# Memory layer: the sample rows of both feature blocks stacked and turned by one transpose

## The chip, the cores and the metric

The kernel runs on one NeuronCore of a Trainium2 chip. The metric is the device time of one execution in microseconds (us), the median of several runs. All inputs, outputs and arithmetic are fp32; matrix products are made from split operands (below).

## The reference, cut to what matters

One inference step of a two-layer decoder runs over 320 tokens: a prompt of 256 tokens and a sample group of 8 sequences with 8 new tokens each (64 tokens). Layer 0 is a gated MLP over chunks, layer 1 is an mLSTM (a matrix memory with 8 heads, key width 128, value width 256), and each layer is followed by a convolutional feed-forward block. The change touches the end of each head of the mLSTM, where its output is normalised over the 256 value features, gated and handed to the output projection:

```
num = w_inter * (q @ C) + sc @ v
den = w_inter * (q @ n) + sum(sc)
h   = num / max(|den|, exp(-m_t))
hn  = (h - mean(h)) * rsqrt(var(h) + EPS) * gn_g      # over the 256 features of a head
y   = (sigmoid(o_pre) * hn) @ w_out
```

## The kernel before, in words

**Layout.** The residual stream lies with features on the 128 partitions and the 320 tokens along the free axis: columns 0 to 255 are the prompt, columns 256 to 319 the sample (`TP` = 256, `T` = 320). Every projection is made of blocks of 128 output features: `block` (L185) multiplies eight 128x128 weight tiles with the 320 token columns. Weights and activations are split in a high part (`wh`, `xh`, `yhb`) and a low part (`wl`, `xl`, `ylb`), and a product is three matmuls: high-high, high-low, low-high. In the memory layer `chunk` (L173) first makes the 16 matmuls with `wh`, then the 8 with `wl`.

**The weight stream.** A list `wq` (L65 to L114) names the weights in the order of their use. `take` (L165) hands out the next one and calls `prefetch` (L120): the raw weight four places ahead is loaded by a DMA of SyncE (SP) into one of four `raw` buffers, and the next one is split in one of three pairs of buffers: ScalarE (ACT) makes `wh` (L154), VectorE (DVE) makes `wl` = `raw` - `wh` (L155).

**The heads.** The loop over 8 heads `h` (L1025) is software-pipelined: in iteration `h`, the projections of head `h` alternate on TensorE (PE) with the remaining steps of head `h`-1. In the order of PE: q block, `inter` (products with the state C), k block, `numer` (the numerators: two PSUM tiles for the prompt rows, one for the sample), first v block, `state_prompt`, `state_sample` 0, second v block, `state_sample` 1, `scores` of head `h`, first o block, **`finish` of head `h`-1**, `state_sample` 2, second o block, `state_sample` 3, `k_nat`, `v_nat` (transposes of k and v), `inter(h, 0)`. In the heads below, "finish(h)" is the step for head `h`; finish(0) to finish(6) stand in iterations 1 to 7, finish(7) after the loop. Beside these stand blocks of the output projection (`early`), wherever their operands are ready.

**The last head.** The output projection's inputs from heads 4 to 7 come late, so three of its blocks are begun in pieces by `begin` (L1016). Weight pieces of 4, 4, 2 and 2 tiles (L101 to L103) are taken in iteration 7 and just behind the loop, and the order of PE there is:

```
h = NH - 1
begin(0)        # 2 tiles
begin(1)        # 2 tiles
inter(h, 1)
for i in (2, 3):
    inter(h, i)
numer(h)
ps = blk()
```

**The step that is changed.** `stats` (L898) has token rows on the partitions. For the two prompt tiles (128 rows each) the numerators stay in PSUM; for the sample, ACT and DVE sum two halves into `ns` (64 rows x 258, SBUF). It computes mean and variance (DVE), a power -1/2 (POOL, L919), a scale `sl` and a bias `nb` (DVE, L922, L926), and then ACT writes the normalised rows to `hn` (128 x 3 x 256): one instruction for each of three token tiles, the third with 64 rows (L929). Rows 64 to 127 of the third tile are zeros, written once (L998). `finish` (L968) turns `hn` back: for each of the two feature blocks `e`, three 128x128 transposes on PE (`tr`, L975) into one PSUM tile `phn`, of which columns 0 to 319 are used; DVE multiplies them with the gate (L977, `y_b`), ACT makes `yhb` (L979), DVE `ylb` (L980).

**What sets the order.** Every matmul and transpose is pinned: PE works in the order of the program. On the other engines and on the DMA queue of SP a list scheduler of the framework decides, when the kernel is built, in which order the instructions are issued; each engine then works through its list strictly in that order, and waits where an operand is not ready. Only a few instructions beside PE's are pinned or told what to follow (`behind_split`, L160; `between`, L1092). PSUM tiles come from two rings: `psm` with three tiles for blocks, `psa` with five for everything else (`phn` among them); a tile of a ring is given out again after its last reader.

Of the kernel before, what the change touches and what calls it, by code (L numbers as in the profile page):

```python
# [10 lines left out]
F32 = mybir.dt.float32  # L11
F32R = mybir.dt.float32r
AF = mybir.ActivationFunctionType
ALU = mybir.AluOpType
MULT, ADD, SUB, MAX = ALU.mult, ALU.add, ALU.subtract, ALU.max

P = 128
EPS = 1e-6
TP = 256
NB, NS = 8, 8  # L20
T = TP + NB * NS
# [6 lines left out]
DV = 256  # L28
# [9 lines left out]
class Net:  # L38
# [576 lines left out]
    def layer_b(self):  # L615
        nc, tc, I, O = self.nc, self.tc, self.I, self.O
# [4 lines left out]
        with ExitStack() as ctx:  # L621
# [276 lines left out]
            def stats(h, between=None):  # L898
                s = S[h]
                num, mv, dn = s.pop("num"), mvs[h % 2], dns[h % 2]  # L900
                ns = hp.tile([64, CW], F32, tag="ns", name="ns", bufs=1)
                nc.scalar.copy(ns, num[2][64:, :CW])
                nc.vector.tensor_tensor(ns, num[2][:64, :CW], ns, op=ADD)
                src = [num[0], num[1], ns]
                bst = hp.tile([P, 3, 6], F32, tag="bstat", name="bstat", bufs=1)
                for t in range(3):
                    n = P if t < 2 else 64
                    nc.vector.bn_stats(bst[:n, t, :], src[t][:n, :DV])
                    nc.vector.bn_aggr(mv[:n, t, :], bst[:n, t:t + 1, :])
                    nc.scalar.activation(dn[:n, t:t + 1], src[t][:n, DV:DV + 1], AF.Abs)  # L910
                rd = hp.tile([P, 3], F32, tag="rd", name="rd", bufs=1)
                nc.vector.tensor_tensor(rd, dn, colsT[:, :, 64 + h], op=MAX)
                nc.vector.reciprocal(rd, rd)
                t1 = hp.tile([P, 3], F32, tag="t1", name="t1", bufs=1)
                nc.vector.tensor_tensor(t1, mv[:, :, 1], rd, op=MULT)
                nc.vector.tensor_tensor(t1, t1, rd, op=MULT)
                nc.vector.tensor_scalar(t1, t1, EPS, None, op0=ADD)
                sl = hp.tile([P, 3], F32, tag="sl", name="sl", bufs=1)
                made = nc.gpsimd.tensor_tensor(sl, t1, self.mhalf.to_broadcast([P, 3]), op=ALU.pow)  # L919
                if between:  # L920
                    between(made)
                mul = nc.vector.tensor_tensor(sl, sl, rd, op=MULT)  # L922
                if between:
                    self.pin(mul)
                nb = hp.tile([P, 3], F32, tag="nb", name="nb", bufs=1)
                nc.vector.scalar_tensor_tensor(nb, mv[:, :, 0], -1.0, sl, op0=MULT, op1=MULT)  # L926
                for t in range(3):
                    n = P if t < 2 else 64
                    nc.scalar.activation(hn[:n, t, :], src[t][:n, :DV], AF.Identity, scale=sl[:n, t:t + 1], bias=nb[:n, t:t + 1])  # L929

            def state_prompt(h):
                s = S[h]
# [35 lines left out]
            def finish(h):  # L968
                s = S[h]
                yh = hp.tile([P, 2, T], F32R, tag="yhb", name="yhb", bufs=6)  # L970
                yl = hp.tile([P, 2, T], F32R, tag="ylb", name="ylb", bufs=6)
                for e in range(2):
                    pt = self.psa.tile([P, 512], F32, tag="pa", name="phn")
                    for t in range(3):
                        self.tr(pt[:, t * P:(t + 1) * P], hn[:, t, e * P:(e + 1) * P], self.ident)  # L975
                    y = self.tp.tile([P, T], F32, tag="yf", name="y_b", bufs=2)
                    nc.vector.scalar_tensor_tensor(y, s["o"][e], 1.0, pt[:, :T], op0=ADD, op1=MULT)  # L977
                    g = gnh[:, 2 * h + e:2 * h + e + 1]
                    nc.scalar.activation(yh[:, e, :], y, AF.Copy, scale=g)  # L979
                    nc.vector.scalar_tensor_tensor(yl[:, e, :], y, g, yh[:, e, :].bitcast(F32), op0=MULT, op1=SUB)  # L980
                    Y[2 * h + e] = (yh[:, e, :], yl[:, e, :])
# [8 lines left out]
            hp = ctx.enter_context(tc.tile_pool(name="hb", bufs=1))  # L990
# [2 lines left out]
            Qz = hp.tile([P, 8 * 136], F32R, name="Qz")  # L993

            Ps = hp.tile([P, P], F32R, name="Ps")
            hn = hp.tile([P, 3, DV], F32, name="hn")
            nc.gpsimd.memset(Ps.bitcast(F32), 0.0)
            nc.gpsimd.memset(hn[64:, 2, :], 0.0)  # L998
            nc.gpsimd.memset(vh[:, :, DV:DV + 1].bitcast(F32), 1.0)
            nc.gpsimd.memset(vh[:, :, DV + 1:].bitcast(F32), 0.0)  # L1000
            nc.gpsimd.memset(vl[:, :, DV:].bitcast(F32), 0.0)
# [23 lines left out]
            for h in range(NH):  # L1025
                if h:
                    qk_epi(h, 0, blk())
                    early(h, 0)
                    if h == 1:
                        inter(0, 0)  # L1030
                        state_split(0, 3)
                    inter(h - 1, 1)
                    qk_epi(h, 1, blk())
                    for i in (2, 3):
                        inter(h - 1, i)
                    numer(h - 1)
                    early(h, 1)
                    ps = blk()
                    with self.behind_split():
                        stats(h - 1)  # L1040
                    v_epi(h, 0, ps)
                    state_prompt(h - 1)
                    state_sample(h - 1, 0)
                    early(h, 2)
                    v_epi(h, 1, blk())
# [7 lines left out]
                if h:  # L1053
                    finish(h - 1)
# [37 lines left out]
            def between(made):  # L1092
                with tc.issue_after(made.ins):
                    k_mask(h)
                o_epi(h, 0, ps)

            stats(h, between)
            state_prompt(h)
            o_epi(h, 1, blk())
            finish(h)  # L1100
            for i in range(4):
                state_sample(h, i)
# [159 lines left out]
```

## Time and profile before

| | before |
|---|---|
| median of 3 runs | 965.59 us (965.24 to 965.87) |
| profiled execution, its own time | 965.17 us |
| its span, first to last instruction | 963.4 us |
| mean granted TensorE clock | 0.997 of full speed |
| transposes into `phn` | 48, six for each head |
| normalised sample rows `hn<-ns` (L929) | 8 of 64x256, 595 ns each |
| gate product `y_b` (L977) | 16 of 128x320, 475 ns each |
| memory layer's heads on PE | about 450 us to 704 us of the span |

A row of a timeline or of the chain reads: start in us from the span's start, duration in us, engine, line, operation, out<-in. Durations of neighbours on an engine overlap, since instructions are pipelined: what one costs its queue is the distance from its start to the next start, here called its pitch. PE is TensorE's matmul and transpose, PEld its weight load, which runs ahead of the matmul that uses it. SPq is the DMA queue of SyncE.

### The profile page before, as it was taken

What the parts mean: (1) busy time and instruction counts of PE and PEld (TensorE: products, weight loads), DVE (VectorE), ACT (ScalarE), POOL (GpSimd) and SP (SyncE); (2) the same over time, 40 slices, a digit from 0 to 9 for tenths busy, and PEclk for the clock granted to TensorE, in tenths of its full rate; (3) what the DMA queues carried; (4) which work ended last, traced back from release to release, by engine and by line L of the source; (5) the groups of instructions that cost most, each with busy time, mean ns of one, the idle gap of its engine ahead of it and who ended that gap; (6) DMA issues with size and microseconds to landing.
All of it is one profiled execution on the core that took longest, in us unless ns stands there. A gap on an engine that the chain in (4) does not pass through costs nothing.

```text
span 963.4 us, 17284 instructions
## 1 busy us (share of the span) xinstructions
PE 954.8 (99%) x6495; PEld 942.1 (98%) x6495; DVE 700.8 (73%) x1364; ACT 518.0 (54%) x946; POOL 114.0 (12%) x288
## 2 busy tenths in 40 slices
PE   9999999999999999999999999999999999999997
PEld 8889999999999999999999999999999999999997
DVE  6766976587777755469999988787887777775443
ACT  7557444455555443358676756565665455444341
POOL 2200000010000000024322212102101000000000
PEclk9999999999999999999999999999999999999998
DMA  8643356544444455564465654554474444445441
GB/s 274 208 145 132 130 153 192 166 135 151 153 154 147 143 166 149 152 225 144 150 200 183 188 189 162 186 171 125 131 239 137 153 154 153 153 138 160 141 139 55
DMA packets 58505, 154.83 MB, mean 161 GB/s; under 512 B 7782, under 2 KB 20326, under 8 KB 58422
## 3 DMA queue, kind: packets, MB, share of 16 engines
q1 hardware_dynamic: 58422, 153.74, 50.3%
q8 instruction: 51, 0.84, 0.4%
q14 instruction: 32, 0.26, 0.1%
HBM read 141.78 MB, written 11.94 MB: 160 GB/s over the span
## 4 chain that ended last, share of the span: by engine, by line
PE 97%; DVE 2%; ACT 1%; issue 0%; DVEq 0%; POOL 0%; ACTq 0%
PE pm L54 81%; PE pv_a L54 6%; PE num L54 3%; PE pcs L54 2%; PE pmix L54 1%; PE psc L54 1%; PE pCp L54 1%; PE pv L57 1%; PE phn L57 1%; DVE wl L155 0%; PE pw L54 0%; PE pc L54 0%; PE pk L57 0%; DVE yo L610 0%; ACT wh L154 0%
## 5 line engine op out<-in xcount | busy, mean ns | idle before, releaser
L154 ACT CAST wh<-raw 128x1024 fp32r<-128x1024 f32 (+3 forms) x256 | 256.9, 1004 | 299.6 <-PE pm L54 150.0
L155 DVE TENSOR_TENSOR wl<-raw,wh 128x1024 fp32r<-128x1024 f32 (+3 forms) x256 | 298.9, 1168 | 116.2 <-ACT wh L154 112.1
L54 PE MATMUL pm<-xh,wh 128*128 128x320 f32 x1216 | 372.3, 311 | 0.0
L54 PE MATMUL pm<-xl,wh 128*128 128x320 f32 x1216 | 370.3, 309 | 0.0
L54 PE MATMUL pm<-xh,wl 128*128 128x320 f32 x1216 | 321.1, 309 | 0.0
L54 PEld LDWEIGHTS pm<-xl,wh 128*128 128x128 f32 x1216 | 228.3, 188 | 0.2
L54 PEld LDWEIGHTS pm<-xh,wh 128*128 128x128 f32 x1216 | 228.3, 188 | 0.2
L54 PEld LDWEIGHTS pm<-xh,wl 128*128 128x128 f32 x1216 | 214.5, 188 | 0.0
L54 PE MATMUL pm<-yh_f,wh 128*128 128x320 f32 x352 | 108.8, 309 | 0.0
L54 PE MATMUL pm<-yl_f,wh 128*128 128x320 f32 x352 | 108.8, 309 | 0.0
L54 PE MATMUL pm<-yh_f,wl 128*128 128x320 f32 x352 | 108.8, 309 | 0.0
L54 PEld LDWEIGHTS pm<-yh_f,wh 128*128 128x128 f32 x352 | 66.1, 188 | 0.0
L54 PEld LDWEIGHTS pm<-yl_f,wh 128*128 128x128 f32 x352 | 66.1, 188 | 0.0
L54 PEld LDWEIGHTS pm<-yh_f,wl 128*128 128x128 f32 x352 | 66.1, 188 | 0.0
L531 DVE SCALAR_TENSOR_TENSOR fcv<-fpad,vecs,fcv 128x336 f32<-128x336 f32 x88 | 49.6, 565 | 2.1 <-ACT fcv L529 0.6
L303 DVE TENSOR_TENSOR xT<-pm,xT 128x320 f32<-128x320 f32 x39 | 19.1, 490 | 33.5 <-PE pm L54 33.1
L54 PE MATMUL pm<-yh_a,wh 128*128 128x320 f32 x128 | 39.6, 310 | 0.0
L54 PE MATMUL pm<-yh_a,wl 128*128 128x320 f32 x128 | 39.5, 309 | 0.0
L54 PE MATMUL pm<-yl_a,wh 128*128 128x320 f32 x128 | 39.5, 309 | 0.0
L533 ACT ACTIVATE fgl<-fcv 128x256 f32<-128x256 f32 x44 | 18.2, 415 | 37.8 <-DVE fcv L531 37.8
L54 PE MATMUL pm<-yhb,wh 128*128 128x320 f32 x128 | 38.1, 311 | 0.0
L54 PE MATMUL pm<-ylb,wh 128*128 128x320 f32 x128 | 37.9, 309 | 0.0
(290 smaller groups left out, 1399.0 us busy)
## 6 DMA issues: line engine op xcount, KB each, us to landing
raw<-in_f_up SPq DMA_DIRECT2D x88, 512.0 KB, 3.3
raw<-in_b_win SPq DMA_DIRECT2D x48, 512.0 KB, 3.6
raw<-in_f_dn SPq DMA_DIRECT2D x32, 448.0 KB, 3.3
C<-in_C SPq DMA_DIRECT2D x32, 258.0 KB, 3.6
raw<-in_a_win SPq DMA_DIRECT2D x16, 512.0 KB, 3.3
raw<-in_a_wo SPq DMA_DIRECT2D x16, 512.0 KB, 3.9
raw<-in_f_dn SPq DMA_DIRECT2D x16, 512.0 KB, 3.5
out_Cs<-C SPq DMA_DIRECT2D x32, 256.0 KB, 2.8
```

Source lines behind the costliest of these rows:

```text
L54: self.pin(self.nc.tensor.matmul(out, lhsT, rhs, start=start, stop=stop, skip_group_check=skip))
L57: self.pin(self.nc.tensor.transpose(out, in_, ident))
L154: self.last_split = self.hold(nc.scalar.copy(wh[:, :kn, :], raw[:, :kn, :]))
L155: self.last_low = nc.vector.tensor_tensor(wl[:, :kn, :], raw[:, :kn, :], wh[:, :kn, :].bitcast(F32), op=SUB)
L303: self.nc.vector.tensor_tensor(x, ps[:, :T], x, op=ADD)
L531: nc.vector.scalar_tensor_tensor(cv, pd[:, i:i + NC], self.vec(w + i * KF), cv, op0=MULT, op1=ADD)
L533: nc.scalar.activation(gl[:, :TP], cv[:, :TP], AF.Gelu_apprx_tanh)
```

## The change

The sample rows of a head are 64 tokens x 256 features. Before, they are one 64x256 tile, padded with zero rows to 128, and cost one transpose in each feature block. After, ACT writes them in two halves into a tile `hs` of 128x128: features 0 to 127 on partitions 0 to 63, features 128 to 255 on partitions 64 to 127. One transpose of `hs` gives both blocks side by side in columns 256 to 383 of the first `phn` tile (`p0`). The second block's gate product is made in two: its 64 sample columns from `p0`, its 256 prompt columns from its own tile. The zero fill is gone.

```diff
@@ stats
-                for t in range(3):
-                    n = P if t < 2 else 64
-                    nc.scalar.activation(hn[:n, t, :], src[t][:n, :DV], AF.Identity, scale=sl[:n, t:t + 1], bias=nb[:n, t:t + 1])
+                for t in range(2):
+                    nc.scalar.activation(hn[:, t, :], src[t][:, :DV], AF.Identity, scale=sl[:, t:t + 1], bias=nb[:, t:t + 1])
+
+                for e in range(2):
+                    nc.scalar.activation(hs[64 * e:64 * e + 64, :], ns[:, e * P:(e + 1) * P], AF.Identity, scale=sl[:64, 2:3], bias=nb[:64, 2:3])
@@ finish
-                    for t in range(3):
+                    for t in range(2):
                         self.tr(pt[:, t * P:(t + 1) * P], hn[:, t, e * P:(e + 1) * P], self.ident)
                     y = self.tp.tile([P, T], F32, tag="yf", name="y_b", bufs=2)
-                    nc.vector.scalar_tensor_tensor(y, s["o"][e], 1.0, pt[:, :T], op0=ADD, op1=MULT)
+                    o = s["o"][e]
+                    if not e:
+                        p0 = pt
+                        self.tr(pt[:, TP:TP + P], hs, self.ident)
+                        nc.vector.scalar_tensor_tensor(y, o, 1.0, pt[:, :T], op0=ADD, op1=MULT)
+                    else:
+                        nc.vector.scalar_tensor_tensor(y[:, TP:], o[:, TP:], 1.0, p0[:, T:384], op0=ADD, op1=MULT)
+                        nc.vector.scalar_tensor_tensor(y[:, :TP], o[:, :TP], 1.0, pt[:, :TP], op0=ADD, op1=MULT)
@@ layer_b
-            hn = hp.tile([P, 3, DV], F32, name="hn")
+            hn = hp.tile([P, 2, DV], F32, name="hn")
+            hs = hp.tile([P, P], F32, name="hs")
             nc.gpsimd.memset(Ps.bitcast(F32), 0.0)
-            nc.gpsimd.memset(hn[64:, 2, :], 0.0)
```

Since the scheduler plans the other engines anew, the change also moves instructions that it does not name. On VectorE, in the iterations of heads 1 to 4 the split `wl` of one weight goes from behind the second o gate to behind the transposed k and v of the head (`kgs`, `vl`, `kgl`, L841 to L849) and the state split `Cl`. In iteration 7 the queue of VectorE behind the last state update reads, before and after:

```
before:  wl(256a) ... y_b, ylb, C, ylb, C C C, wl(256b), wl(1024), kgs, vl, vl, Cl, kgl, vl, wl(1024), kgl, ns
after:   ... y_b, y_b(64), ylb, y_b(256), C C, ylb, C C, wl(256a), kgs, vl, vl, kgl, Cl, vl, wl(256b), kgl, wl(1024), wl(1024), ns
```

Here wl(256a) and wl(256b) are the low parts of the two-tile pieces that `begin(0)` and `begin(1)` use behind the loop, and wl(1024) those of the two o blocks of head 7.

## The prediction

> **What bounds the kernel.** I read the page first, then PE's waits, the chain of waits and the timelines of the engines around the change. The page:
>
> ```profile
> span 963.4 us, 17284 instructions
> PE 954.8 (99%) x6495; PEld 942.1 (98%) x6495; DVE 700.8 (73%) x1364; ACT 518.0 (54%) x946; POOL 114.0 (12%) x288
> PE 97%; DVE 2%; ACT 1%; issue 0%; DVEq 0%; POOL 0%; ACTq 0%
> ```
>
> PE is busy 99% of the span and 97% of the chain that ended last. So a PE instruction taken away is time won, and work on another engine costs nothing until PE waits for it. The list of PE's waits between 470 and 700 us is empty: in the heads PE never stands still for long. VectorE is the next to bind there: in the timeline by stretches it is busy 27.8 of 30 us from 500 to 530 us. The chain shows what the transposes cost on PE, at finish(0) and, in its second stretch, at finish(7):
>
> ```profile
> 473.79 0.66 PE phn L57 x6
> 474.45 0.46 PE pcs L54 x4
> ```
>
> ```profile
> 695.45 0.71 PE phn L57 x6
> 696.17 1.87 PE pcs L54 x16
> ```
>
> The reader is to see 0.66 us for six transposes, 0.11 each, and 0.71 at finish(7): there PE lost 0.05 us to a wait.
>
> **1. Transposes.** Six become five in each of 8 heads: 8 x 0.11 = **0.88 us less** on PE.
>
> **2. ACT writes the sample rows in two instructions.** At finish(0) ACT's timeline reads:
>
> ```profile
> 472.13 1.02 ACT L929 ACTIVATE hn<-num,nb,sl 128x256 f32<-128x256 f32 x2 [2.09 <-DVE nb L926]
> 473.05 0.60 ACT L929 ACTIVATE hn<-ns,nb,sl 64x256 f32<-64x256 f32 x1
> 473.54 0.55 ACT L787 ACTIVATE w<-pMb,cols 128x128 f32<-128x128 f32 x2
> ```
>
> The 64x256 instruction takes 0.60 us with a pitch of 0.49. No row has its 64x128 form. The same operation at line 434 takes 805 ns for 512 columns and 588 ns for 256, 0.85 ns a column, so 128 columns fewer save 0.11: 0.49 us, pitch 0.38. The second half then ends at 473.05 + 0.38 + 0.49 = 473.92 instead of 473.65. Bounds: with the 128x128 row of `w` (0.36, pitch 0.24) 473.65, nothing lost; with the pitch unchanged at 0.49, 474.03. I take 473.92, from the row of the same operation. PE loads the third operand at 473.74: at finish(0) it waits 0.2 us (0 to 0.3). At finish(1) `hn` ends at 502.02 and PE begins at 503.29, finish(2) to (5) have 2 us and more, and finish(6) has 0.5 (675.72 and 676.22): nothing there. ACT itself has 0.27 us more per head and is idle for 2 us before each `hn`.
>
> **3. The divided gate product, the zero fill, PSUM.** On DVE 320 columns (pitch 0.39) become 64 and 256 (0.13 and 0.33, the pitches of lines 746 and 745): 0.07 us per head, under the 2 us that DVE is idle per head; without that cover 0.6 us in all. The first `phn` tile is read 0.2 us longer; its place in the ring of five comes back with the first `pv` tile, at 508.89 in iteration 2, when `y_b` has ended at 506.5: covered by 2 us. POOL's fill (306 ns) lies off the path.
>
> **4. The new order of VectorE.** This is where I expect the loss. In iterations 1 to 4 one `wl` is moved behind instructions worth about 3.7 us (in iteration 2: C C 0.9, `kgs` 0.4, three `vl` 1.3, two `kgl` 0.5, `Cl` 0.65). There it was made at 510.90 and PE first loads it at 521.88; in iteration 1 at 482.75 and 492.20. The least cover, 9.4 us, stays at 5.7: nothing lost. SP's raw loads move behind loads of C, by up to 7 us; their gap from issue to `wh` is 11 us or more in these heads, and a load lands in 3.6: nothing.
>
> At the last head there is no such cover:
>
> ```profile
> 681.74 0.47 DVE L958 SCALAR_TENSOR_TENSOR C<-C,dec,pcs 128x256 f32<-128x256 f32 x1
> 682.13 1.55 DVE L155 TENSOR_TENSOR wl<-raw,wh 128x256 fp32r<-128x256 f32 x2
> 683.71 0.36 DVE L841 SCALAR_TENSOR_TENSOR kgs<-pk,cols,kgt 64x128 fp32r<-64x128 f32 x1
> 684.10 0.87 DVE L824 SCALAR_TENSOR_TENSOR vl<-pv,rc,vh 128x256 fp32r<-128x256 f32 x2
> 684.90 0.68 DVE L868 TENSOR_TENSOR Cl<-C,Ch 128x516 fp32r<-128x516 f32 x1
> 685.50 0.34 DVE L849 SCALAR_TENSOR_TENSOR kgl<-pk,cols,kgh 128x128 fp32r<-128x128 f32 x1
> 685.76 0.47 DVE L824 SCALAR_TENSOR_TENSOR vl<-pv,rc,vh 128x256 fp32r<-128x256 f32 x1
> ```
>
> ```profile
> 683.39 0.46 PE L54 MATMUL pm<-yhb,wl 128*128 128x320 f32 x2
> 683.69 0.31 PE L54 MATMUL pm<-yhb,wh 128*128 128x320 f32 x1
> ...
> 684.28 0.46 PE L54 MATMUL pm<-yhb,wl 128*128 128x320 f32 x2
> ```
>
> Before, wl(256b) is the first of the two at 682.13, ends at 682.55, and PE needs it at 684.13 (weight load of the matmul at 684.28). After, it stands behind `kgs`, three `vl`, one `kgl` and `Cl`. I walk DVE's new queue with the pitches of these rows: `y_b` 678.24 (as before), Pl 678.63, Ps 679.11, `y_b`(64) 679.25, `ylb` 679.58 (its `yhb` ends at 679.52), `y_b`(256) 680.04, C C 680.37, `ylb` 681.15, C C 681.61, wl(256a) 682.4 to 682.8 (needed at 683.14: in time), `kgs` 682.8, `vl` 683.2, `vl` 683.6, `kgl` 684.0, `Cl` 684.3, `vl` 684.95, wl(256b) **685.35 to 685.8**. PE, 0.11 earlier by finish(6), asks at 684.02: a pause of 1.8 us. From below: the last `vl` waits for `vh` of ACT, whose queue cannot start `kgt` before 682.06 (its `wh` before that waits for a buffer that PE frees at 680.99) and has `kgs`, two `vh`, `kgh` and `Ch` ahead, so `vh` ends at 684.65 and wl(256b) at 685.45 at the earliest: 1.45. From above, with 0.3 for waits along that queue: 2.1. I take **1.7 us**, near the walk. `inter` and `numer` behind it find `Cl` and `vl` ready, so nothing more is lost there; SP's raw load of the next piece (768 columns) goes from 676.92 to about 683.0 behind two state stores, lands at 686.4, and delays `wh` and `ns` on ACT to 687.3, before PE's numerators (now 688.2).
>
> What is late next is finish(7). The statistics start behind two wl(1024) about 1.1 us later than before, PE comes 1.6 us later, and the second half of `hs` costs 0.27: it is ready about 0.25 us before PE asks, and the 0.05 us lost there before are won.
>
> **Clock.** A pause of PE could slow it. The timeline by stretches has a granted clock of 1.00 from 420 to 425 us, where PE stands still for 0.8 us, but 0.71 from 955 to 960, where it is busy for 2.4 of 5. A pause of 1.7 us lies between the two. The Trainium skill (TensorE: Matmul & The Clock Gate, "Part 1: The HAM clock gate") says that the clock is halved after a whole idle window of about 3.4 us; by that rule this pause leaves it alone, and both rows agree, but no row shows 1.7 us.
>
> **Sum**: -0.88 + 0.2 + 1.7 - 0.05 = **+0.97 us** against the profiled execution's 965.17 (span 963.4 and 1.77 around it, unchanged): 966.1. The median of the runs, 965.59, lies 0.42 above that execution; I put the predicted time half of this higher: **966.4**.
>
> **The rivals**, on the same footing (965.4 before):
>
> - *No pause* (0.14): wl(256b) is in time. Against it stands the strict order of DVE's queue and of PE's; for it, that the walk is 1.8 us long and a `vl` that ran earlier would shorten it. Then finish(7) is not covered: `hs` 0.27 later, wait 0.3. -0.88 + 0.2 + 0.3: 965.0.
> - *Only the transposes count* (0.06): no pause, and ACT's halves cost no more than the one: 965.4 - 0.9 = 964.5.
> - *VectorE becomes the bound of the heads* (0.12, slower): busy 93% from 500 to 530 us, it is now asked to wait more often, since Pl stands behind the o gate and behind ACT's `Ph`, which in iterations 2 to 6 stands behind a `wh`. This decides if more than the 5.7 us of cover is lost. One us over it in each of four heads: +4 on the forecast, 970.4. Against it: the moves come to 3.7 us, and idle time does not add up from head to head.
> - *The clock falls* (0.06, slower): one block of 24 matmuls (3.5 us in the chain) at half the clock, as in the last stretch of the span (0.50): +3.5, 969.9.
> - *The forecast* (0.62): 966.4, its own range from the bounds (finish(0) 0 to 0.3, pause 1.45 to 2.1, median or profiled time) 965.5 to 967.2.
>
> The range that should hold 8 in 10 takes in the two lower rivals and the start of the upper: **964.4 to 968.3**. About 0.2%, 1.9 us, is what a measurement of this kernel can tell from no change: faster 0.02, same 0.77, slower 0.21 (both slower rivals and the end of the forecast).
>
> **What would show it.** `phn` 40 times, five in 0.55 us. PE idle once between 680 and 690 us, for 1.5 to 2 us, released by DVE at line 155; no other wait in the heads but 0.2 us at finish(0). `hs` at about 0.49 us. Granted clock 1.00 up to 955 us. The forecast is wrong if PE shows no wait at `begin(1)`, or waits in iterations 1 to 4, or if `hs` takes 0.36 us or less.

## The result, and the profile after

| | before | after |
|---|---|---|
| median of 6 runs | 965.57 us (965.24 to 966.07) | 969.52 us (969.19 to 970.34) |
| profiled execution, its own time | 965.17 us | 969.4 us |
| its span | 963.4 us | 967.7 us |
| mean granted TensorE clock | 0.997 | 0.997 |

The ratio is 1.0042, with a 95% interval of 1.0032 to 1.0053: 3.95 us slower. The forecast was 966.4, its range 964.4 to 968.3: the time lies above the range, and the change is slower by more than 0.2%, to which the forecast gave a chance of 0.21.

The page of the changed kernel, its first lines and the shares of its chain:

```profile
span 967.7 us, 17280 instructions
PE 956.4 (99%) x6487; PEld 941.8 (97%) x6487; DVE 701.8 (73%) x1372; ACT 519.7 (54%) x954; POOL 114.4 (12%) x287
PE 83%; DVE 9%; ACT 4%; issue 1%; DMA 1%; POOL 1%; DVEq 0%; ACTq 0%
```

PE still looks 99% busy, with 8 instructions fewer. But the chain that ended last was 97% PE and is now 83%: 9% of it is VectorE. PE's waits between 460 and 705 us (what it waited for, us in total, times, longest), empty before, say where PE stands now:

```profile
PE pm L54 <- DVE wl L155: 1.6, 1, 1.6
PE num L54 <- DVE C L960: 0.8, 3, 0.3
```

The first is the forecast pause. The second is new: in three heads PE waits for `C` of VectorE. It does not need the value (`num` reads `Ch`, `Cl` and `Qz`); it needs the PSUM tile of the ring `psa` that `C` is the last to read. To see all of it, the start of the same PE instruction is compared in the two traces, and the difference followed through the heads:

| stretch of PE | lost, us | forecast |
|---|---|---|
| up to the scores of head 1 (start of the program, not touched by the change) | 0.36 | 0 |
| to the first product with C of head 1: finish(0) | +0.41 | +0.1 |
| heads 1 to 4, to the scores of head 5 | **+2.13** | **-0.33** |
| finish(4) to finish(6), to the last head's products | -0.33 | -0.33 |
| `begin(1)`: the pause | +1.94 | +1.7 |
| finish(7) and the rest | -0.2 | -0.16 |

Without the first row the sum is 3.95. Of the 0.41, 0.22 is finish(0), and 0.19 is a wait at the first `num` of head 1 (480.41), 0.14 us after the end of `C`, as with the three waits listed. The steps of the forecast are there nearly as priced, and one stretch misses by 2.5 us: iterations 1 to 4, where the forecast saw nothing lost.

What is different there can be seen in the order of VectorE and GpSimd. First the kernel before, in iteration 2:

```profile
511.71 0.36 DVE L841 SCALAR_TENSOR_TENSOR kgs<-pk,cols,kgt 64x128 fp32r<-64x128 f32 x1
512.10 0.48 DVE L824 SCALAR_TENSOR_TENSOR vl<-pv,rc,vh 128x256 fp32r<-128x256 f32 x1
512.15 1.90 POOL L853 TENSOR_TENSOR kgz<-kgs,mk 128x1024 fp32r<-128x1024 f32 x1 [8.14 <-DVE kgs L841]
512.58 0.35 DVE L849 SCALAR_TENSOR_TENSOR kgl<-pk,cols,kgh 128x128 fp32r<-128x128 f32 x1
512.84 0.86 DVE L824 SCALAR_TENSOR_TENSOR vl<-pv,rc,vh 64x256 fp32r<-64x256 f32 x2
513.63 0.33 DVE L849 SCALAR_TENSOR_TENSOR kgl<-pk,cols,kgh 128x128 fp32r<-128x128 f32 x1
513.88 0.72 DVE L868 TENSOR_TENSOR Cl<-C,Ch 128x516 fp32r<-128x516 f32 x1
```

The same place in the changed kernel:

```profile
513.10 0.36 DVE L841 SCALAR_TENSOR_TENSOR kgs<-pk,cols,kgt 64x128 fp32r<-64x128 f32 x1
513.49 0.87 DVE L824 SCALAR_TENSOR_TENSOR vl<-pv,rc,vh 128x256 fp32r<-128x256 f32 x2
513.54 1.90 POOL L853 TENSOR_TENSOR kgz<-kgs,mk 128x1024 fp32r<-128x1024 f32 x1 [7.39 <-DVE kgs L841]
514.28 0.33 DVE L849 SCALAR_TENSOR_TENSOR kgl<-pk,cols,kgh 128x128 fp32r<-128x128 f32 x1
514.58 1.41 DVE L868 TENSOR_TENSOR Cl<-C,Ch 128x516 fp32r<-128x516 f32 x1
515.91 0.34 DVE L849 SCALAR_TENSOR_TENSOR kgl<-pk,cols,kgh 128x128 fp32r<-128x128 f32 x1
```

`kgz` is GpSimd's mask product of 1.90 us, which starts as soon as `kgs` is there. The new order does not only move a `wl`, as told in "The change": it also moves `Cl` forward. Before, three `vl` and two `kgl` stood between `kgs` and `Cl`; now two `vl` and one `kgl` do. Before, `Cl` came 1.73 us after the start of `kgz`, 0.17 before its end, and took 0.72. After, it comes 1.04 us after that start and takes **1.41**, until 515.99, where `kgz` ends at 515.44: 0.86 us beside `kgz` and 0.55 behind it. Before, too, `Cl` ended 0.55 us behind `kgz`. `kgl`, which has one operand in PSUM, runs beside `kgz` at its usual 0.33. The long `Cl` (both operands in SBUF) is there in all four of these heads (484.21, 514.58, 544.94, 575.31) and nowhere before. That this is the cause is shown in experiment 6; it was not the first suspect.

### The profile page after: what moved, and what is told of

Read it like the earlier page. It is cut to its first block, busy times and chain, and to the rows that moved or that the text cites. A ratio compares the mean times of both kernels' runs of the same rounds, so it can differ in the third digit from the quotient of the medians.

```text
span 967.7 us, 17280 instructions
## 1 busy us (share of the span) xinstructions
PE 956.4 (99%) x6487; PEld 941.8 (97%) x6487; DVE 701.8 (73%) x1372; ACT 519.7 (54%) x954; POOL 114.4 (12%) x287
## 4 chain that ended last, share of the span: by engine, by line
PE 83%; DVE 9%; ACT 4%; issue 1%; DMA 1%; POOL 1%; DVEq 0%; ACTq 0%
PE pm L54 72%; PE pv_a L54 6%; DVE wl L155 2%; PE num L54 1%; DVE bcv L753 1%; ACT wh L154 1%; DVE C L960 1%; PE pmix L54 1%; DMA out_Cs<-C 1%; PE pcs L54 1%; DVE Cl L868 1%; POOL sl L919 1%; DMA C<-in_C 1%; DVE Pl L311 0%; DVE qs L757 0%
## 5 line engine op out<-in xcount | busy, mean ns | idle before, releaser
L303 DVE TENSOR_TENSOR xT<-pm,xT 128x320 f32<-128x320 f32 x39 | 19.1, 490 | 30.2 <-PE pm L54 29.7
```

Of the source, the lines that this page charges most:

```text
L303: self.nc.vector.tensor_tensor(x, ps[:, :T], x, op=ADD)
```

## The experiments

"Pace" below is the distance from one `dec` of VectorE (L797, once per head) to the next, in the heads 1 to 4. PE alone needs 29.69 us per head before (finish(1) to finish(2); 29.65 and 29.66 beside it) and, less one transpose, 29.58 after. The pace of VectorE was 28.94 before (29.17 in the first of three intervals) and is 30.35 after: before, it was 0.75 shorter than PE's, and after it is 0.77 longer, so that PE waits for VectorE.

**1. The parts, one by one.** Four kernels. The changed one with a sixth transpose put back (read by nobody); before with the divided gate product alone; before with the sample rows in two instructions alone; before with five transposes alone (the sixth left out, so that the second block takes the first block's sample columns).

```diff
sixth_transpose, in finish:
+                    if e:
+                        self.tr(pt[:, TP:TP + P], hs, self.ident)
row_halves_alone, in stats:
-                for t in range(3):
+                for t in range(2):
...
+                for e in range(2):
+                    nc.scalar.activation(hn[:64, 2, e * P:(e + 1) * P], ns[:, e * P:(e + 1) * P], ...)
five_transposes_alone, in finish:
-                    for t in range(3):
+                    for t in range(2 if e else 3):
```

> The changed kernel with a sixth transpose put back, into columns that nobody reads: PE has the work of before, ACT, VectorE and the reads those of after. The schedule that comes of it keeps the late low half of the 256-column weights at the last head and ACT's weight split ahead of Ph, but has no state split between the scale and the bias of the statistics in iterations 2 to 4. Theory (the loop through VectorE and ACT is over PE's 29.7 us, and most of the excess is that state split of 0.6 us): the loop falls to 29.8, so finish(0) +0.33, pause +1.94, heads +0.2 in iteration 1 and 0.1 in each of the next three: 968.3. Rival 1 (ACT's two half writes alone make the loop long): the loop stays at 30.36, the transposes of heads 0 and 5 to 7 cost 0.44 again: 970.0. Rival 2 (only PE's own queue counts): 0.88 above the changed kernel, 970.4.

> The kernel before, with nothing but the second gate product divided into 64 and 256 columns; its rows, its six transposes and its order in the heads stay. Theory (VectorE's own extra 0.07 us per head is not what lengthened the loop): 0 to 0.3 us above before, 965.6 to 965.9. Rival 2 (VectorE at 93% has no room, so that any instruction more costs the whole of what was lost): 0.7 us in each of four heads, 968.4.

> The kernel before, with nothing but the sample rows written by two instructions of 128 columns in place of one of 256; the schedule that comes of it has ACT's weight split ahead of Ph as in the changed kernel, but no state split between scale and bias in iterations 2 to 4, and the low half of the last head's weights early. Theory: finish(0) waits 0.33, the loop of the heads comes to 29.8 against PE's 29.7, so 0 to 0.1 in each of four: 965.9 to 966.3, no pause at the last head. Rival 1 (ACT's halves alone lengthen the loop by all 0.67): 965.6 + 0.3 + 2.7 = 968.6.

> The kernel before with one transpose of the six left out and nothing else on ACT: the sample columns of the second block are taken from the first block's tile, so that they hold the first block's normalised rows, and the second gate product is divided. The schedule has a state split between scale and bias in iteration 2 alone, Ph ahead of the weight split, the low half early. Theory: 0.11 saved in the heads that PE bounds, 0.08 in those of the loop (the cover of psc), less 0.3 in iteration 2: 964.9 to 965.2. Rival 2 (PE alone counts): 965.6 - 0.88 = 964.7.

| kernel | median | ratio to before (95%) | pace | long `Cl` |
|---|---|---|---|---|
| sixth_transpose | 969.77 | 1.0037 (1.0023 to 1.0051) | 29.77 | 0 |
| gate_product_alone | 965.74 | 1.0003 (0.9994 to 1.0011) | 28.99 | 0 |
| row_halves_alone | 966.03 | 1.0006 (0.9997 to 1.0014) | 29.44 | 0 |
| five_transposes_alone | 965.61 | 1.0001 (0.9992 to 1.001) | 29.82, then 29.00 | 1 |

The gate product costs nothing and the halves cost PE nothing; so no part does it alone. But row_halves_alone lengthens VectorE's pace by 0.50, two thirds of its slack: 0.28 between `nb` and `dec`, where ACT writes the halves, and 0.22 at `Pl`, which waits longer for ACT's `Ph` (0.47 for 0.25), since `Ph` now stands behind a `wh`. Five transposes alone missed the expected 964.9 to 965.2: in iteration 1 one `Cl` falls into `kgz` (1.41), and that interval is 29.82 where it was 29.17. sixth_transpose came out as the first rival said, but for another reason. Its heads lose 0.34 only, without a long `Cl`; the rest is the pause, and a clock that fell behind it. Its timeline by stretches (stretch, its us, busy us of PE, PEld, DVE, ACT, POOL with instructions, granted clock, DMA share, GB/s):

```profile
690.00:692.00 2.00, 2.00 (x11) 2.00 (x11) 1.64 (x4) 0.75 (x3) 0.00 (x0) 0.50 0.49 137
```

PE is busy for all of the 2 us and makes 11 matmuls. The clock is 0.50 from 689.1 to 692.5, so 3.4 us hold half as much work: about 1.7 us, without which the median would be near 968.1, by this estimate. The fastest of its five executions took 967.88.

**2. The first theory, and how it fell.** In the changed kernel a `Cl` stands between VectorE's scale `sl` and bias `nb`, for which ACT waits before `hn`. The theory: this late bias lengthens the loop VectorE, ACT, VectorE. bias_before_split puts two `Cl` behind `nb` in iterations 1 to 4; the other way round, split_between_in_before and one_split_between_in_before put one between them in the kernel before, the first with its other `Cl` behind `t`.

```diff
bias_before_split, in layer_b:
-                        state_split(h, i)
+                        with tc.issue_after(self.nb_made.ins) if h in (1, 2, 3, 4) and i < 2 else nullcontext():
+                            state_split(h, i)
...
one_split_between_in_before, in stats (mid makes one Cl behind sl, in iterations 2 to 4):
-                nc.vector.scalar_tensor_tensor(nb, mv[:, :, 0], -1.0, sl, op0=MULT, op1=MULT)
+                with tc.issue_after(mid(mul).ins) if mid else nullcontext():
+                    nc.vector.scalar_tensor_tensor(nb, mv[:, :, 0], -1.0, sl, op0=MULT, op1=MULT)
```

> The changed kernel with one order written out: in iterations 1 to 4 the splits of the first two pieces of C are issued behind nb, so that no Cl stands between the scale and the bias of the statistics. All else, with the late low half at the last head and ACT's weight split ahead of Ph, stays as in the changed kernel. Theory (that Cl is most of the loop's excess): the stretch of heads 0 to 4 falls by 2.0 to 2.4 us, 969.5 - 2.2 = 967.3, or 1.6 more where the clock falls behind the pause at the last head. Rival (ACT's halves and the order of Ph and Pl keep the loop at 30.1 or more): at most 1.0 us won, 968.5.

> The kernel before, its arithmetic untouched, with the order of the changed kernel put into its VectorE queue in iterations 2 to 4: a Cl stands between the scale and the bias of the statistics (one more Cl comes to stand between the bias and dec). Six transposes, one row write, one gate product, Ph and the last head as before. Theory (the place of Cl alone lengthens the loop through VectorE, whose cover at psc is 0.08 us): 0.5 to 1.1 us in each of three heads, 967.1 to 968.8. Rival 1 (ACT's two half writes are needed for the loop to bind): 965.6 to 966.1.

> The kernel before, its arithmetic untouched, with exactly one Cl in each of iterations 2 to 4 moved from ahead of the last bn_aggr to between scale and bias; nothing else of VectorE's queue changes. Theory (VectorE's own pace from one dec to the next is 28.94 us in the kernel before, 0.75 under PE's 29.69; the moved Cl makes it 29.5, which still fits): PE loses nothing, 965.5 to 965.8, the pace from dec to dec is 29.5 and the cover of psc, 0.08 in iteration 1, stops growing by 0.74 a head. Rival (the move costs PE by itself, since psc has only 0.08 of cover): 967 or more. Rival (the move costs VectorE nothing): pace 28.9.

bias_before_split ran in 968.01 (967.04 to 969.46; ratio 1.0025, 1.0015 to 1.0034) for an expected 967.3: the heads lose nothing any more, as expected, and a new wait of 0.8 for a `wl` at 715 us took part of it back. But the two kernels that bring the suspected order into the kernel before lose nothing: 965.79 beside 965.70 (1.0, 0.9991 to 1.0009) where 967.1 to 968.8 was expected, and 965.59 beside 965.72 (0.9999, 0.999 to 1.0007), with a pace of 28.96, where 29.5 was expected. The bias was not it. In bias_before_split all four `Cl` of 1.4 us are still there; three `Cl` now stand behind `nb` and fill the time in which VectorE waits at `dec`, which goes from 1.43 to 0. It repaid the loss in another place.

**3. ACT's weights.** Another suspect for the same loop: `Ph` of ACT stands behind a `wh`. ph_before_weights lets the weights be split only behind `Ph` in iterations 1 to 4.

```diff
+                if 0 < h < 5:
+                    self.SPLIT_AHEAD = 0
...
+                if 0 < h < 5:
+                    self.SPLIT_AHEAD = 1
+                    with tc.issue_after(self.p_made[0].ins), tc.issue_after(self.p_made[1].ins):
+                        self.prefetch(0, self.used + 1)
```

> The changed kernel with a third order written out: in iterations 1 to 4 ACT's weight split and the low half that stood ahead of Ph are asked for behind the split of the masked scores, so that Pl comes ahead of the o gate again. Cl stays between scale and bias in iterations 2 to 4 (in iteration 1 the schedule moves it away), and the late low half at the last head stays. Theory (this order is a part of the loop's excess, 0.2 us a head): 0.7 in the heads and up to 0.5 in iteration 1, 968.3 to 968.8. Rival (Cl is all of it): only iteration 1 gains, 969.0 to 969.3.

970.75 (1.0058, 1.0045 to 1.007) for an expected 968.3 to 968.8, or 969.0 to 969.3 by the rival: a miss for both. No `Cl` is long there, and PE waits for the weights instead:

```profile
PE pm L54 <- ACT wh L154: 3.4, 4, 2.0
PE pm L54 <- DVE wl L155: 1.6, 1, 1.6
```

**4. The pause alone.** low_half_before_keys makes the late wl(256b) ahead of the keys of the last head; both_orders has this and bias_before_split.

```diff
-                k_nat(h)
+                if last:
+                    self.prefetch(0, self.used + 2)
+                    with tc.issue_after(self.last_low.ins):
+                        k_nat(h)
+                else:
+                    k_nat(h)
```

> The changed kernel with one other order written out: at the last head the second 256-column low half is asked for ahead of the key gate kgs, so that it stands behind the state updates as in the kernel before. The heads stay as in the changed kernel. Theory: the pause of 1.95 us goes and nothing waits in its place, 969.5 - 1.95 = 967.6, and the times of single runs lie within 1 us, since no pause is left behind which the clock could fall. Rival (finish(7) is late next and gives back what its cover was): 968.1. Rival (the next split then stands behind it and PE waits there): 969.

> Both orders written out: Cl behind nb in iterations 1 to 4, and the low half ahead of the keys at the last head. Theory (the two losses are separate and add up): 969.5 - 2.2 - 1.95 = 965.4, the time of before, because the five transposes' 0.88 is spent on finish(0) (0.33) and on 0.07 to 0.1 a head that the loop through VectorE and ACT still lacks. Rival (only the transposes and finish(0) are left): 965.5 - 0.88 + 0.33 = 965.0. Rival (one hides the other): over 966.5.

969.74 (1.0044, 1.003 to 1.0057) and 967.89 (1.0025, 1.0016 to 1.0033), 2.1 and 2.5 us above what was expected (967.6 and 965.4). The waits of the first:

```profile
PE num L54 <- DVE C L960: 0.8, 3, 0.3
PE phn L57 <- ACT hs L931: 0.6, 1, 0.6
PE phn L57 <- ACT hn L928: 0.3, 1, 0.3
PE num L54 <- DVE Cl L868: 0.3, 1, 0.3
```

The pause is gone and its worth is given back: by PE's starts 0.39 at the products with `Cl` and 1.48 at finish(7). Two wl(1024) of 2.35 us, and on ACT a `wh` that waits 0.80 for its load, stand ahead of `ns` there. With PE in the pause they had been hidden. both_orders has the same three waits and no wait for `C`.

**5. Half of the sample rows on GpSimd.** If ACT's second half is on the loop, another engine can write it. The third puts two `Cl` of every head but the last behind the last `kgl`, the fourth is the changed kernel with all four `Cl` of heads 2 to 7 behind `nb` (its halves on ACT), and the second has the order of the fourth with the half on GpSimd.

```diff
gpsimd_half:
-                for e in range(2):
-                    nc.scalar.activation(hs[64 * e:64 * e + 64, :], ns[:, e * P:(e + 1) * P], ...)
+                nc.scalar.activation(hs[:64, :], ns[:, :P], AF.Identity, scale=sl[:64, 2:3], bias=nb[:64, 2:3])
+                nc.gpsimd.tensor_scalar(hs[64:, :], ns[:, P:DV], sl[:64, 2:3], nb[:64, 2:3], op0=MULT, op1=ADD)
```

> The changed kernel with the second half of the sample rows written by GpSimd beside ACT, in place of ACT's second instruction. The schedule that comes of it has Cl between scale and bias in iterations 1 and 2 alone, Ph ahead of ACT's split from iteration 2 on, and the low half early at the last head. No row of any run prices GpSimd's write. Theory (ACT's extra 0.27 us a head and the order are the loss): 965.6 - 0.88 + 0.4 in iteration 2 = 965.1, if GpSimd's write ends with ACT's; each 0.1 us that it ends later costs 0.1 at finish(0) and at finish(7). Rival (the write on GpSimd is over 1 us and becomes the late operand of the transposes): 966.5 or more.

> Both: the second half of the sample rows on GpSimd, and Cl behind nb from iteration 2 on. Theory: every wait that the change brought is gone, what stays is the transposes' 0.88 less up to 0.1 a head in the loop: 964.7 to 965.1, less than either kernel. Rival (GpSimd's write is late): 966 or more. Rival (something of the order at the last head is left): 966.5.

> The changed kernel with the second half of the sample rows on GpSimd, and the splits of the third and fourth piece of C issued behind kgl, so that no Cl starts beside kgz. Theory: no wait is left in the heads, PE's work alone counts: 965.65 - 0.88 + 0 to 0.3 at finish(7) = 964.8 to 965.1. Rival (the two Cl that now follow one another delay the rows behind them): 965.5 or more.

> The changed kernel with Cl issued behind nb from iteration 2 on, iteration 1 as it is. The schedule that comes of it at the last head has the second 256-column low half early, as in the kernel before, and ACT's split behind Ph. Theory (the order, and not the work, is what the change cost): the heads at PE's pace, finish(0) +0.33, finish(7) +0.3 for the two half writes, 0.1 a head in iterations 2 to 4, and 0.88 won: 965.6 - 0.88 + 0.33 + 0.3 + 0.3 = 965.65, the time of before. Rival (the last head loses its 2 us whichever low half comes first, as with the low half ahead of the keys): 967.3 to 967.9.

| kernel | median | ratio to before (95%) | what follows |
|---|---|---|---|
| gpsimd_half | 964.88 | 0.9992 (0.9983 to 1.0001) | no wait of PE in the heads; one long `Cl`, pace then 28.92 |
| with `Cl` behind `nb` | 965.20 | 0.9994 (0.9986 to 1.0003) | no wait of PE in the heads; nothing more gained |
| split_behind_keys | 965.64 | 1.0 (0.9991 to 1.0008) | the rival's time: PE waits 0.5 for a `wl` at 713 us |
| later_heads | 966.39 | 1.0007 (0.9998 to 1.0016) | no pause, but finish(7) waits 0.6 for `hs` |

gpsimd_half is the fastest of all, 0.7 to 0.8 below before, with an interval that still takes in no change. With it the scheduler's order has no pause at `begin(1)`.

**6. The cause put to the test.** By now the long `Cl` was the suspect, and it can be taken away without touching an order: changed_without_mask is the changed kernel without the mask product `kgz` in heads 1 to 4, whose matmuls use the masked keys of head 0; VectorE's, ACT's and PE's queues are those of the changed kernel. mask_twice_in_before is the opposite: before, with the mask product made twice in these heads, so that GpSimd is busy when `Cl` comes.

```diff
changed_without_mask:
-                if h < NH - 1:
+                if h < NH - 1 and not 0 < h < 5:
                     k_mask(h)
mask_twice_in_before:
                     k_mask(h)
+                    if 0 < h < 5:
+                        k_mask(h)
```

> The changed kernel with GpSimd's kgz (1.90 us) left out in heads 1 to 4, where the state updates then use head 0's masked keys; the queues of VectorE and ACT are those of the changed kernel, instruction by instruction. Theory (Cl is held up by kgz, 0.70 us a head): Cl 0.70, VectorE's loop 29.66 against PE's 29.58, 2.5 to 2.8 us won: 966.7 to 967.0, with the pause at the last head as it was. Rival (ACT's two half writes, or the order as such, make the loop): 969.0 to 969.5.

> The kernel before with kgz made twice, one behind the other, in heads 1 to 4; VectorE's queue is that of the kernel before, instruction by instruction, with Cl behind both kgl, 1.73 us after the first kgz starts. Theory: the second kgz holds up Cl until it ends, 3.8 us after the first began: Cl 1.4 to 2.1 us longer, VectorE's loop 28.94 + 1.4 to 2.1 = 30.3 to 31.0 against PE's 29.69, in four heads with 0.08 us of cover at first: 2.4 to 5.2 us lost, 968 to 971. Rival (GpSimd's work costs VectorE nothing): 965.7.

**967.32** (966.93 to 967.87; 1.0018, 1.0009 to 1.0027) for changed_without_mask: 2.2 us of the 3.95 are gone. That is somewhat less than the 2.5 to 2.8 expected, and it comes from the heads: from the scores of head 1 to those of head 5, PE loses 0.37 us against before, where the changed kernel lost 2.54. VectorE's timeline at the same place:

```profile
513.23 0.33 DVE L849 SCALAR_TENSOR_TENSOR kgl<-pk,cols,kgh 128x128 fp32r<-128x128 f32 x1
513.53 0.69 DVE L868 TENSOR_TENSOR Cl<-C,Ch 128x516 fp32r<-128x516 f32 x1
514.15 0.35 DVE L849 SCALAR_TENSOR_TENSOR kgl<-pk,cols,kgh 128x128 fp32r<-128x128 f32 x1
```

`Cl` takes 0.69 in the same place of the same queue, the pace falls from 30.35 to 29.65, and of PE's waits one line is left:

```profile
PE pm L54 <- DVE wl L155: 1.6, 1, 1.6
```

mask_twice_in_before ran in 967.94 (1.0022, 1.0013 to 1.0031), just under the expected 968 to 971, and not by way of `Cl`: that slipped in between the two products, and what was held was the `wl` behind it (timeline of iteration 2):

```profile
513.60 4.20 POOL L855 TENSOR_TENSOR kgz<-kgs,mk 128x1024 fp32r<-128x1024 f32 x2 [8.14 <-DVE kgs L841]
515.33 0.72 DVE L870 TENSOR_TENSOR Cl<-C,Ch 128x516 fp32r<-128x516 f32 x1
516.43 2.45 DVE L155 TENSOR_TENSOR wl<-raw,wh 128x1024 fp32r<-128x1024 f32 x1
```

2.45 us instead of 1.21, and the two products take 4.20 together where twice 1.90 is 3.80: GpSimd stood still as well. PE then waits for VectorE in three heads (1.0 us in all: `psc`, which does not read `C` either, for `C`). So work on GpSimd, for which PE never waits here, slows the kernel through VectorE's queue. The Trainium skill (SBUF — State Buffer, "SBUF: two separate sides") describes this: VectorE and GpSimd share access to SBUF as an exclusive lock; an instruction of VectorE that reads two operands from SBUF and one of GpSimd shut each other out, and the one that starts first keeps the other waiting until it is done. The traces agree: 1.41 for 0.70, 2.45 for 1.21, and no loss for `kgl` and `vl`, which read one operand from PSUM. GpSimd loses as well: its half of the sample rows in experiment 5 takes 0.45 us alone and 1.28 to 1.32 beside a `wl` of VectorE.

**7. How long a pause has to be.** Extra copies of a subtraction (2 and 4, written to scratch) ahead of the late wl(256b) of the changed kernel.

```diff
+            if i == self.wq_late:
+                for _ in range(2):
...
+                        d = nc.vector.tensor_tensor(scr, raw[:, :kn, :], wh[:, :kn, :].bitcast(F32), op=SUB)
```

> The changed kernel with two more VectorE instructions of 256 columns (0.38 us each), whose results nobody reads, ahead of the late low half of the last head: PE's pause there grows from 1.95 to 2.7 us. Theory (the clock falls behind a pause of about 2 us or more, according to where it lies in a window of the monitor): half the clock for 3.4 us behind it, 969.5 + 0.75 + 1.7 = 972.0, in most of the runs. Rival (the clock falls only after a pause of over 3.4 us, and in the run with the sixth transpose it had another cause): 970.3, granted clock 1.00.

> The same with four such instructions: the pause grows to 3.5 us. Theory and rival both have the clock fall here for 3.4 us or more: 969.5 + 1.5 + 1.7 = 972.7. If the clock stays at 1.00, 971.0, neither holds.

971.63 (1.006, 1.0047 to 1.0074) and 974.25 (1.0088, 1.0073 to 1.0104): 2.1 and 4.7 us more than the changed kernel. The single executions lie 1.8 and 1.9 us apart. The stretch behind the pause in the profiled ones, first with 2, then with 4 copies:

```profile
690.00:692.00 2.00, 1.95 (x15) 1.95 (x16) 2.00 (x2) 0.84 (x1) 0.00 (x0) 1.00 0.23 68
```

```profile
694.00:696.00 2.00, 2.00 (x11) 2.00 (x11) 0.73 (x3) 0.44 (x2) 0.00 (x0) 0.50 0.53 148
```

In these executions a pause of 3.13 us left the clock at 1.00, and one of 4.04 halved it from about 689.4 to 696.2 (pauses are counted from the start of the last matmul ahead of them to the start of the next).

## Why the prediction was wrong

**The step that failed** is in part 4, on iterations 1 to 4: "The least cover, 9.4 us, stays at 5.7: nothing lost." It took the instructions that the `wl` now stands behind at their old durations and asked only whether this `wl` still comes in time for PE, and it does; no `wl` is late there. It did not ask what those instructions meet in the new order. `Cl` stands one `vl` and one `kgl` nearer to `kgs`, the end of `kgs` starts GpSimd's `kgz`, and `Cl`, priced at 0.65, takes 1.41 beside it. The forecast had 0 for this; it measured 2.2 (969.52 less 967.32). The trace of before held the price, in the last head, in rows that the prediction did not read:

```profile
691.60 1.90 POOL L853 TENSOR_TENSOR kgz<-kgs,mk 128x1024 fp32r<-128x1024 f32 x1
691.66 1.85 DVE L922 TENSOR_TENSOR sl<-sl,rd 128x3 f32<-128x3 f32 x1
```

`sl`, three elements on each partition, takes 1.85 us, where it takes 0.16 in other heads, and it ends 0.01 us behind `kgz`.

**What made these 0.70 us per head count** are two further steps.

- "ACT itself has 0.27 us more per head and is idle for 2 us before each `hn`" took a wait for slack, and 0.27 was too little. That idle time ends with `nb` of VectorE, and VectorE then waits for ACT's `w` behind `hn`: one loop. VectorE's rows in iteration 2 to 3 of before, and then of after:

```profile
529.27 0.16 DVE L926 SCALAR_TENSOR_TENSOR nb<-mv,sl 128x3 f32<-128x3 f32 x1
...
532.24 0.17 DVE L797 COPY dec<-pMb 128x8 f32<-128x8 f32 x1 [0.85 <-ACT w L787]
```

```profile
532.27 0.15 DVE L926 SCALAR_TENSOR_TENSOR nb<-mv,sl 128x3 f32<-128x3 f32 x1
...
535.77 0.17 DVE L797 COPY dec<-pMb 128x8 f32<-128x8 f32 x1 [1.43 <-ACT w L787]
```

  From `nb` to `dec` it was 2.97 and is 3.50. ACT's rows in between, before and after, show where the 0.53 comes from:

```profile
530.38 0.59 ACT L929 ACTIVATE hn<-ns,nb,sl 64x256 f32<-64x256 f32 x1
530.87 0.41 ACT L771 COPY vTb<-pm 128x320 f32<-128x320 f32 x1
```

```profile
533.37 0.99 ACT L931 ACTIVATE hs<-ns,nb,sl 64x128 f32<-64x128 f32 x2
534.39 0.43 ACT L771 COPY vTb<-pm 128x320 f32<-128x320 f32 x1
```

  The whole had a pitch of 0.49; the two halves together have 1.02. The forecast had 0.38 for each. In row_halves_alone, where both halves go to partitions 0 to 63, it is 0.385 each; in the changed kernel the second half goes to partitions 64 to 127, and it is 0.50 and 0.52. Why is not shown. The rest of the growth lies between `dec` and `nb`: 25.97 before, 26.85 after, 26.15 in changed_without_mask. So of the 1.41 by which the pace grows, 0.53 is ACT's halves, 0.70 is the long `Cl`, and 0.18 is left for the gate product (0.06 by itself) and the longer wait for `Ph` (0.22 in row_halves_alone); no run shows why these two come to less than their sum.
- "idle time does not add up from head to head" was wrong. VectorE was 0.75 us faster per head than PE, and what it gained it kept: the time by which `C` came before PE asked for it grew from 0.08 to 0.83 and 1.54 from head to head. The loop's own length is what PE's has to be compared with, not the idle share of a stretch: VectorE, at 27.8 busy of 30 us, had 0.75 to give, and the change took 1.41. Without the long `Cl` the pace is 29.65, 0.07 over PE's (changed_without_mask); the long `Cl` alone would make it 28.94 + 0.70 = 29.64, by estimate; both together pass it by 0.77. The rival "VectorE becomes the bound of the heads" was the right one, and its chance of 0.12 too low, though it too put the decision on the cover of 5.7 us.

**What was right.** The transposes: five in 0.55 us, so 0.11 less in each head. In the chain:

```profile
605.91 0.55 PE phn L57 x5
```

This was won only where PE sets the pace, in finish(4) to finish(6), 0.33 in three. `hs`: 0.49 each, as worked out from line 434, though not with the pitch. finish(0): PE waits for `hs`, as forecast, but 0.33 for 0.2 (0 to 0.3), since the second half starts 0.12 later than the forecast pitch had it. The pause: in its place, for the reason given, of 1.64 us by the releaser's wait and 1.94 by PE's starts; the forecast was 1.7, between 1.45 and 2.1. PE's row:

```profile
688.65 0.56 PE L54 MATMUL pm<-yhb,wl 128*128 128x320 f32 x2 [1.64 <-DVE wl L155]
```

finish(7) lost nothing behind the pause, and the clock stayed at 1.00 there. "No pause" and "only the transposes count" did not happen in the changed kernel; gpsimd_half, without a pause, ran in 964.88, near the 965.0 of the first. Had the heads cost -0.33, the measured sum would have been 1.5 us instead of 3.95, inside the range.

What stays open: why the scheduler's orders put the `wl` where they do, and whether an order exists that keeps the transposes' whole 0.88; the best one found keeps it within what can be measured.

## What to carry to other kernels

Beside a bound engine, work out the pace of each loop of other engines per round, waits included, and compare it with the bound engine's own: 0.75 us of 29.7 was all that could be spent here, though the lists of waits were empty. When a reordering moves instructions, look at what runs on GpSimd in their new place: a VectorE instruction with both operands in SBUF can double there. A wait that is removed is worth only what the next late operand leaves of it; low_half_before_keys took away 1.94 us and got nothing.

## What the runs showed of the hardware

- A VectorE instruction with two operands in SBUF and a GpSimd instruction that reads SBUF shut each other out. On VectorE: 128x516 in 1.41 us for 0.70, 128x1024 in 2.45 for 1.21, 128x3 in 1.85 for 0.16. On GpSimd: 64x128 in 1.28 to 1.32 for 0.45 beside one `wl`, and in 2.33 beside two `Cl` and a `wl` in a row (gpsimd_half_bias_before_split). The loser is shown as busy, so no list of waits has it.
- The length of a pause does not settle whether the clock falls: 1.95 us (the changed kernel) and 3.13 us left it at 1.00, 2.12 us (sixth_transpose) halved it for 3.4 us and 4.04 us for 6.8 us. The Trainium skill (TensorE: Matmul & The Clock Gate, "Part 1: The HAM clock gate") asks for a whole idle window of about 3.4 us, not tied to the start of the pause. The 3.13 and the 4.04 us agree with this, the 2.12 us does not, and the measurement decides.
- ACT's write of 64x128 with scale and bias takes 0.49 us. Two in a row have a pitch of 0.385 each when both write partitions 0 to 63 (row_halves_alone), and of 0.50 and 0.52 when the second writes partitions 64 to 127 (the changed kernel).
